# Differential attention: scaling each output tile one step later in the written order

## The chip, the cores and the metric

The kernel runs on one core of one Trainium2 chip. The metric is the device time of one execution in microseconds (us); lower is better. Every engine (TensorE, VectorE, ScalarE, GpSimd, and SyncE, which issues transfers) works through its own queue in order; semaphores tie them together.

## The reference

A two-layer decoder trunk for 512 tokens of width 1024, in float32. Layer 0 runs latent attention and differential attention side by side, then a gated feed-forward network with a short convolution; layer 1 runs two other kinds of attention and such a network again. What matters here is differential attention in layer 0: 4 heads, queries in 4 blocks of 128, value width 128.

```python
def probs(qb, kf):
    s = jnp.einsum('bhqd,bhkd->bhqk', qb, kf).astype(jnp.float32) * scale + bias
    return jax.nn.softmax(jnp.where(causal, s, -jnp.inf), axis=-1)

p = probs(a1, k1) - lam * probs(a2, k2)
return jnp.einsum('bhqk,bhkd->bhqd', p.astype(v.dtype), v)
...
o_diff = diff_attention(dq[:, :, 0], dq[:, :, 1], dk[:, :, 0], dk[:, :, 1], dv, lam,
                        alibi_slopes(DIFF_HEADS))
o_diff = rms_norm(o_diff, subln_g) * (1.0 - lam_init)
return jnp.concatenate([heads_last(o_mla), heads_last(o_diff)], axis=-1) @ w_out
```

Each row of 128 outputs of a head is divided by its root mean square and multiplied by a gain before the output projection.

## The kernel before

Nearly all the work is matrix products in three parts: each float32 matrix is split into a rounded high part (ScalarE's cast, L83) and the rest (VectorE's subtraction, L84), and `mm3` (L316) multiplies high by high, high by low and low by high. TensorE is kept supplied with such products while the attention runs.

Differential attention is written as a pipeline over 16 units, one for each head and query block, in the order of L1355: head by head, blocks 3, 2, 0, 1. The loop at L1361 has 20 steps, numbered n from 0. Within it, the order of the text is the order of the instructions on TensorE, VectorE, ScalarE and GpSimd (`manual_schedule`, L1360); nothing reorders them. In a step n:

- `score` (L1227): TensorE makes the two score blocks of unit n; VectorE adds the position bias and takes the minimum (L1246).
- a weight tile is loaded and split (`W.ahead` or `W2.next`, L1367 to L1372: L83 and L84).
- `exps` (L1250): ScalarE takes the exponentials and their sums.
- `fill` (L1344): TensorE works through ready-made products, `plan[n][0]` of them here and `plan[n][1]` further down.
- `turn` (L1263): TensorE transposes the combined probabilities of unit n - 1 (L883), ScalarE copies them out (L886).
- `value` (L1266): for unit n - 2, TensorE multiplies by the values (L1271), ScalarE scales the result into the head's tile `otok` (L1272) and sums its squares (L1275), and GpSimd makes the inverse root r: an addition (L1277) and a power (L1278). The constant it adds, `epsp`, is set once by GpSimd (L1209).
- a move: GpSimd issues one transfer of a chain that adds up feed-forward weights in DRAM (`sum_steps`, L147; the issue is L163). An earlier part of that chain, without steps of the loop in between, stands ahead of the loop in GpSimd's queue (`make_sums`, L1058 and L1059).
- `norm` (L1282): VectorE scales an earlier unit's output tile by its r and the gain, in place (L1285).
- `combine` (L1256): VectorE forms the difference of the two probability blocks of unit n (L1258 to L1260).
- in steps 7, 11, 15 and 19, `finish` (L1288): TensorE transposes the four scaled tiles of a head (L1292), ScalarE and VectorE split the result (L226, L227) for the output projection.

The steps in which an operation of a unit stands are set only by the offsets in the loop's text. `r` lies in one of four buffers of the tag `rr` (L1276), `otok` in one of two (L1229).

Of the kernel before, what the change touches and what calls it, by code (L numbers as in the profile page):

```python
# [97 lines left out]
def trunk(tc, A, out):  # L98
# [3 lines left out]
    with ExitStack() as top:  # L102
# [98 lines left out]
        units = []  # L201
# [18 lines left out]
        def gain(name, row):  # L220
            g = glob.tile([P, D], F32, tag="gain", name="gain", bufs=2)
            nc.sync.dma_start(g[:], A[name][row:row + 1, :].partition_broadcast(P))
            return g
# [628 lines left out]
        def even():  # L852
            with ExitStack() as es:
# [38 lines left out]
                with ExitStack() as e1:  # L892
# [197 lines left out]
                    def score(p2, i):  # L1090
                        w = (i + 1) * P
                        ps = [bank("s", "sps")[:, :w] for _ in range(2)]
                        for z in range(2):
                            h = 2 * p2 + z
                            PE.matmul(ps[z], mq[h][:, i * P:(i + 1) * P], mk[h][:, :w], start=True, stop=True)
                        st = sc.tile([P, 8], F32, tag="st", name="st", bufs=3)
                        s = [sc.tile([P, S], F32, tag="s", name="s", bufs=4)[:, :w] for _ in range(2)]
                        for z in range(2):
                            DVE.tensor_tensor_reduce(out=s[z], in0=ps[z], in1=mmask[:, 384 - i * P:S], scale=1.0,
                                                     scalar=3e38, op0=ALU.add, op1=ALU.min, accum_out=st[:, z:z + 1])  # L1100
                        for z in range(2):
                            ACT.activation(s[z], s[z], AF.Exp, bias=st[:, z:z + 1], scale=-1.0,
                                           accum_out=st[:, 2 + z:3 + z])
                        return s, st
# [10 lines left out]
                    def turn(p2, i, s):  # L1115
                        for z in range(2):
                            if i == 0:
                                pts[p2, z] = sc.tile([P, 1280], F32, tag="pt", name="pt", bufs=3)
                            pt = pts[p2, z]
                            tp = bank("tn"[z], "tpp", 4, P)  # L1120
                            for j in range(i + 1):
                                PE.transpose(tp[:, j], s[z][:, j * P:(j + 1) * P], ident[:])
                            for j in range(0, i + 1, 2):
                                n = min(2, i + 1 - j)
                                c = off[j] + (i - j) * P
                                d = off[j + 1] - off[j] - P
                                o = pt[:, c:c + P] if n == 1 else pt[:, c:c + 2 * d].rearrange(
                                    "p (a b) -> p a b", a=2)[:, :, 0:P]
                                t = tp[:, j] if n == 1 else tp[:, j:j + 2]
                                if z:  # L1130
                                    ACT.copy(o, t)
                                else:
                                    DVE.tensor_copy(o, t)

                    def value(p2):
                        o = bank("o", "o")
                        for j in range(NT):
                            for y in range(2):
                                h = 2 * p2 + y
                                PE.matmul(o[y * 64:(y + 1) * 64, j * P:], mv[:, j, h * 64:(h + 1) * 64],  # L1140
                                          pts[p2, y][:, off[j]:off[j + 1]], start=(j == 0), stop=(j == NT - 1))
                        return lambda: split(oM[0][:, p2], oM[1][:, p2], o)
# [19 lines left out]
                    units = [(p2, i) for p2 in range(4) for i in range(NT)]  # L1162
# [3 lines left out]
                    def fill(n):  # L1166
                        for _ in range(n):
                            next(fills.pop(0))
# [81 lines left out]
                def exps(a):  # L1250
                    e, st = a
                    for z in range(2):
                        ACT.activation(e[z], e[z], AF.Exp, bias=st[:, 1 - z:2 - z], scale=-1.0,
                                       accum_out=st[:, 3 - z:4 - z])

                def combine(a):  # L1256
                    e, st = a
                    DVE.reciprocal(st[:, 4:6], st[:, 2:4])  # L1258
                    DVE.scalar_tensor_tensor(st[:, 6:7], st[:, 4:5], st[:, 3:4], neglam[:], ALU.mult, ALU.mult)
                    DVE.scalar_tensor_tensor(e[0], e[1], st[:, 6:7], e[0], ALU.mult, ALU.add)  # L1260
                    return e[0], st
# [20 lines left out]
                def norm(h, i):  # L1282
                    def f(r):
                        o = otoks[h][:, i]
                        DVE.scalar_tensor_tensor(o, o, r[:, 0:1], subg[:], ALU.mult, ALU.mult)  # L1285
                    return f

                def finish(h):  # L1288
                    def f(_):
                        tp = bank("t", "tpo", NT, P)  # L1290
                        for i in range(NT):
                            PE.transpose(tp[:, i], otoks[h][:, i], ident[:])  # L1292
                        split(oD[0][:, h], oD[1][:, h], tp.rearrange("p a b -> p (a b)"))
                    return f
# [60 lines left out]
                units = [(h, i) for h in range(4) for i in (3, 2, 0, 1)]  # L1355
                moves = sum_steps(0, range(3, 5))
                scored, turned_, valued = {}, {}, {}
                plan = ((6, 2),) + ((2, 2),) * 11 + ((2, 1),) * 4 + ((1, 0), (1, 1), (1, 2), (0, 2))
                depth, W.depth = W.depth, 0
                with tc.manual_schedule(engines={PE.engine, DVE.engine, ACT.engine, POOL.engine}):  # L1360
                    for n in range(len(units) + 4):  # L1361
                        if n < len(units):
                            a = score(*units[n])
                        if n == 8:
                            nc.sync.dma_start(g_post[:], A["ev_post_g"][0:1, :].partition_broadcast(P))
                            g_next = gain("ffn_pre_g", 0)
                        if n in (3, 6, 9):  # L1367
                            wout.append(W2.next())
                        elif len(wout) < 4:
                            W.ahead(min(len(W.made) + 1, W.pos - len(busy) + 5))  # L1370
                        elif n == 15:
                            W.ahead(W.pos + 4)  # L1372
                        if n < len(units):
                            exps(a)
                        fill(plan[n][0])
                        if n >= 1 and n - 1 < len(units):
                            turned_[n - 1] = turn(*units[n - 1])(scored.pop(n - 1))
                        if n >= 2 and n - 2 < len(units):
                            valued[n - 2] = value(*units[n - 2])(turned_.pop(n - 2))
                            if moves:  # L1380
                                moves.pop(0)()
                        fill(plan[n][1])
                        if n >= 3 and n - 3 < len(units):
                            norm(*units[n - 3])(valued.pop(n - 3))
                        if n < len(units):
                            scored[n] = combine(a)
                        if n >= 7 and n % 4 == 3:
                            finish(n // 4 - 1)(None)
                    fill(1000)
# [36 lines left out]
        def odd(xnT, pending, order):  # L1426
            xh, xl = xnT
            with ExitStack() as es:
# [411 lines left out]
                return nx, [turn_next, turns[1]]  # L1840

        xnT = even()
        xnT = ffn(0, *xnT, False)
        xnT = odd(*xnT)
# [104 lines left out]
```

## Time and profile before

| what | us |
| --- | --- |
| median of 3 runs | 1118.72 |
| lowest and highest run | 1118.53 to 1124.62 |
| the profiled execution | 1120.18 |
| its span, first to last instruction | 1118.1 |
| first and last start of the scaling L1285 | 144.3 to 201.6 |

The profile is of one execution. Its views give each instruction's start from the beginning of the span; rows of a timeline read start, duration, engine, line, operation, output<-inputs, the tile's size, a count, and in brackets the idle time of the engine ahead of it with the instruction that ended it. PE is TensorE's matrix product, PEld its weight load, DVE VectorE, ACT ScalarE, POOL GpSimd, SP SyncE. A releaser is inferred from semaphores, so a wait for several things is put down to the last of them. TensorE's granted clock was 0.999 of full speed over the span.

### The profile page before, as it was taken

The numbers are of one execution on the slowest core, as the hardware profiler recorded it, in microseconds if no ns is written. First come the engines' busy times: TensorE is split into PE (matmuls) and PEld (weight loads), VectorE is DVE, ScalarE is ACT, GpSimd is POOL, SyncE is SP. The second block draws the span as 40 slices with busy tenths as digits, with TensorE's granted clock in tenths as the row PEclk, the third lists the DMA queues.
The fourth block names the chain that finished last, engine by engine and source line by source line (L and its number), as shares of the span: only waits on it lengthen the run. The fifth ranks groups of instructions, "written<-read, shape, count | busy, mean of one in ns | idle before, by whom it ended". The sixth has DMA issues, their size and how long they took to land.

```text
span 1118.1 us, 18149 instructions
## 1 busy us (share of the span) xinstructions
PE 1105.9 (99%) x6792; PEld 961.6 (86%) x6792; DVE 898.6 (80%) x1509; ACT 641.9 (57%) x1091; POOL 126.2 (11%) x241
## 2 busy tenths in 40 slices
PE   9999999999999999999999999999999999999997
PEld 8876667898999999887888877888999999988876
DVE  6667676488899999999874566677899999999896
ACT  5555576346666665556543554565466666656562
POOL 2311143320000000000032111013200000000002
PEclk9999999999999999999999999999999999999999
DMA  8788898457556555354738999947656565535461
GB/s 289 239 227 228 224 283 219 126 181 199 170 180 196 173 187 180 123 179 150 245 95 280 289 293 289 238 115 201 201 155 199 173 187 191 173 126 164 151 207 75
DMA packets 72599, 218.02 MB, mean 195 GB/s; under 512 B 10048, under 2 KB 11200, under 8 KB 64320
## 3 DMA queue, kind: packets, MB, share of 16 engines
q1 hardware_dynamic: 61248, 147.53, 39.9%
q0 software_dynamic: 9920, 67.12, 24.0%
q10 hardware_dynamic: 1344, 2.23, 0.6%
q8 instruction: 53, 0.87, 0.3%
q14 instruction: 34, 0.28, 0.1%
HBM read 209.47 MB, written 73.43 MB: 253 GB/s over the span
## 4 chain that ended last, share of the span: by engine, by line
PE 76%; DMA 10%; DVE 8%; issue 4%; ACT 1%; POOL 1%; SPq 0%; POOLq 0%; DVEq 0%; ACTq 0%
PE u L320 12%; PE u L318 12%; PE u L319 12%; DMA ws<-in_ffn_up_q 5%; DVE wl L84 3%; DMA ws<-ws 3%; PE apt L318 3%; PE apt L319 3%; PE apt L320 3%; PE acc L318 3%; PE acc L320 2%; PE acc L319 2%; PE ao L318 2%; PE ao L320 2%; PE ao L319 2%
## 5 line engine op out<-in xcount | busy, mean ns | idle before, releaser
L84 DVE TENSOR_TENSOR wl<-wraw,wh 128x1024 fp32r<-128x1024 f32 x246 | 298.8, 1220 | 39.8 <-ACT wh L83 39.0
L83 ACT CAST wh<-wraw 128x1024 fp32r<-128x1024 f32 x246 | 254.8, 1047 | 111.8 <-PE u L319 24.4
L320 PE MATMUL u<-xh,wl 128*128 128x256 f32 (+1 forms) x640 | 195.0, 305 | 0.0
L318 PE MATMUL u<-xh,wh 128*128 128x256 f32 (+1 forms) x640 | 194.9, 305 | 0.0
L319 PE MATMUL u<-xl,wh 128*128 128x256 f32 (+1 forms) x640 | 194.8, 304 | 0.0
L320 PEld LDWEIGHTS u<-xh,wl 128*128 128x128 f32 x640 | 122.3, 191 | 5.5 <-DVE wl L84 0.7
L319 PEld LDWEIGHTS u<-xl,wh 128*128 128x128 f32 x640 | 122.3, 191 | 5.0
L318 PEld LDWEIGHTS u<-xh,wh 128*128 128x128 f32 x640 | 122.3, 191 | 4.9
L318 PE MATMUL u<-gh,wh 128*128 128x256 f32 x384 | 108.7, 283 | 0.0
L320 PE MATMUL u<-gh,wl 128*128 128x256 f32 x384 | 108.6, 283 | 0.0
L319 PE MATMUL u<-gl,wh 128*128 128x256 f32 x384 | 108.6, 283 | 0.0
L318 PE MATMUL acc<-wh,gh 128*128 128x512 f32 (+1 forms) x234 | 90.5, 389 | 0.6 <-DVE uu L689 0.6
L319 PE MATMUL acc<-wl,gh 128*128 128x512 f32 (+1 forms) x234 | 90.9, 388 | 0.0
L320 PE MATMUL acc<-wh,gl 128*128 128x512 f32 (+1 forms) x234 | 90.7, 387 | 0.0
L233 POOL TENSOR_TENSOR rv<-ms,epst 128x1 f32<-128x1 f32 x39 | 12.8, 329 | 632.2 <-ACT junk L285 287.0
L482 ACT ACTIVATE y<-u,cw 128x512 f32<-128x512 f32 x88 | 67.8, 777 | 26.8 <-PE u L320 26.8
L319 PEld LDWEIGHTS u<-gl,wh 128*128 128x128 f32 x384 | 73.7, 192 | 0.1
L318 PEld LDWEIGHTS u<-gh,wh 128*128 128x128 f32 x384 | 73.6, 192 | 0.1
L320 PEld LDWEIGHTS u<-gh,wl 128*128 128x128 f32 x384 | 73.7, 192 | 0.0
L163 POOL DMA_DIRECT2D ws<-in_ffn_up_q x72 | 51.6, 718 | 161.8 <-DMA ws<-ws 75.0
L488 DVE SCALAR_TENSOR_TENSOR y<-u,cw,y 128x510 f32<-128x510 f32 x88 | 65.6, 747 | 2.2
L486 DVE SCALAR_TENSOR_TENSOR y<-u,cw,y 128x511 f32<-128x511 f32 x88 | 65.1, 744 | 0.9 <-ACT y L482 0.9
(374 smaller groups left out, 2495.6 us busy)
## 6 DMA issues: line engine op xcount, KB each, us to landing
ws<-in_ffn_up_q POOLq DMA_DIRECT2D x48, 768.0 KB, 12.3
wraw<-ws SPq DMA_DIRECT2D x128, 256.0 KB, 3.0
wraw<-in_ffn_up_q SPq DMA_DIRECT2D x96, 256.0 KB, 2.9
wraw<-in_ffn_w_down SPq DMA_DIRECT2D x44, 512.0 KB, 3.5
ws<-ws POOLq DMA_DIRECT2D x16, 768.0 KB, 14.2
ws<-in_ffn_up_q POOLq DMA_DIRECT2D x24, 512.0 KB, 6.2
wraw<-in_ffn_w_up SPq DMA_DIRECT2D x24, 512.0 KB, 4.5
wraw<-in_od_w_dqk SPq DMA_DIRECT2D x12, 512.0 KB, 10.3
```

The source lines that it names most:

```text
L83: self.nc.scalar.copy(h[:, :w], raw[:, :w])
L84: self.nc.vector.tensor_tensor(l[:, :w], raw[:, :w], h[:, :w].bitcast(F32), ALU.subtract)
L163: nc.gpsimd.dma_start(tiles[j][c][:].rearrange(wide, q=4), src.rearrange(wide, q=4), accum_op=op, max_dma_last_dim=8192)
L233: POOL.tensor_tensor(v[:, :n], ms, epst[:, :n], ALU.add)
L318: PE.matmul(o, lh, rh, start=first, stop=False, skip_group_check=more)
L319: PE.matmul(o, lh, rl, start=False, stop=False, skip_group_check=more)
L320: PE.matmul(o, ll, rh, start=False, stop=last, skip_group_check=more)
L482: ACT.activation(y[:, z], u[z], AF.Identity, bias=c[:, 3:4], scale=c[:, 2:3])
L486: DVE.scalar_tensor_tensor(y[:, z, 1:], u[z][:, :S - 1], c[:, 1:2], y[:, z, 1:], ALU.mult, ALU.add)
L488: DVE.scalar_tensor_tensor(y[:, z, 2:], u[z][:, :S - 2], c[:, 0:1], y[:, z, 2:], ALU.mult, ALU.add)
```

## The change

The scaling `norm` of unit n - 3 stood in step n; now it is that of unit n - 4. It stands at the same place within a step, between the second `fill` and `combine`. The first scaling moves from step 3 to step 4, the last from step 18 to step 19, where it stands just ahead of the last `finish`. The condition on the upper end is dropped, since the loop has 20 steps and n - 4 is always below 16. Nothing that is computed changes.

```diff
                         fill(plan[n][1])
-                        if n >= 3 and n - 3 < len(units):
-                            norm(*units[n - 3])(valued.pop(n - 3))
+                        if n >= 4:
+                            norm(*units[n - 4])(valued.pop(n - 4))
                         if n < len(units):
                             scored[n] = combine(a)
                         if n >= 7 and n % 4 == 3:
                             finish(n // 4 - 1)(None)
```

On VectorE the scaling of step 3 disappears and one more stands at the end; ScalarE, GpSimd and SyncE issue the same instructions in the same order. On TensorE only semaphore waits move, at three of the four finishes. The head's last unit, 4h + 3, was scaled in step 4h + 6, the step before its finish; it is now scaled in step 4h + 7, the step of its finish.

## The prediction

> **What bounds the kernel now.** I read the page's busy shares and its chain first, then what the scaling line L1285 waits for, then the timelines of VectorE, GpSimd and TensorE around the longest of those waits. Steps are numbered n = 0 to 19 as in the loop at L1361; unit n is scored in step n, and r(n) is the root that GpSimd makes for its output tile in step n + 2.
>
> ```profile
> PE 1105.9 (99%) x6792; PEld 961.6 (86%) x6792; DVE 898.6 (80%) x1509; ACT 641.9 (57%) x1091; POOL 126.2 (11%) x241
> PE 76%; DMA 10%; DVE 8%; issue 4%; ACT 1%; POOL 1%; SPq 0%; POOLq 0%; DVEq 0%; ACTq 0%
> ```
>
> TensorE is busy for 1105.9 of 1118.1 us, so 12.2 us is all that any reordering could save, over the whole program. The change lies in one stage; what counts is where TensorE stands still there. The answer on line L1285 (its count, its minimum, median and maximum in ns, and what its engine waited for):
>
> ```profile
> L1285 DVE SCALAR_TENSOR_TENSOR otok<-otok,rr,subg x16: 341/348/353, 144.3 to 201.6; 128x128 f32<-128x128 f32 x16
> its engine sat idle before it (us, times) until:
>   POOL rr L1278: 8.7, 4
> ```
>
> Four of sixteen scalings hold VectorE up, 8.7 us in all. The first is the longest. VectorE's timeline there (start, duration, operation; in brackets the idle time ahead and its releaser):
>
> ```profile
> 139.68 1.22 DVE L84 TENSOR_TENSOR wl<-wraw,wh 128x1024 fp32r<-128x1024 f32 x1
> 144.27 0.35 DVE L1285 SCALAR_TENSOR_TENSOR otok<-otok,rr,subg 128x128 f32<-128x128 f32 x1 [3.36 <-POOL rr L1278]
> 144.53 0.16 DVE L1258 RECIPROCAL st<-st 128x2 f32<-128x2 f32 x1
> 144.98 0.48 DVE L1260 SCALAR_TENSOR_TENSOR s<-s,st 128x256 f32<-128x256 f32 x1
> 145.38 0.68 DVE L1246 CUSTOM_DVE_ANT_0 s<-sps,dist 128x512 f32<-128x512 f32 x1
> ```
>
> Behind the waiting scaling of unit 0 stands the combine of step 3, whose last instruction (L1260) ends at 144.98 + 0.48 = 145.46. TensorE transposes that result in step 4:
>
> ```profile
> 144.27 0.39 PE L320 MATMUL aqk<-xh,wl 128*128 128x512 f32 x1
> 145.62 0.41 PE L883 MATMUL tpp<-ident,s 128*128 128x128 f32 x2 [0.95 <-DVE s L1260]
> ```
>
> So a VectorE wait of 3.36 us becomes a TensorE wait of 0.95 us. Why r(0) is late shows on GpSimd's timeline:
>
> ```profile
> 136.12 0.53 POOL L163 DMA_DIRECT2D ws<-ws  x1 [8.78 <-DMA ws<-in_ffn_up_q]
> 142.43 0.79 POOL L163 DMA_DIRECT2D ws<-in_ffn_up_q  x1 [5.77 <-PE aqk L320]
> 142.95 0.37 POOL L1209 MEMSET epsp<- 128x1 f32 x1
> 143.41 0.18 POOL L1277 TENSOR_TENSOR st<-st,epsp 128x1 f32<-128x1 f32 x1
> 143.67 0.56 POOL L1278 TENSOR_TENSOR rr<-st,mhalf 128x1 f32<-128x1 f32 x1
> ```
>
> GpSimd issues the weight sums one behind the other, each waiting for the one before to land. The issue at 142.43 adds to the tile that the copy issued at 136.12 fills, so it waits for that landing, whatever releaser the bracket names. Only then comes the constant, the addition and the power: r(0) is there at 143.67 + 0.56 = 144.23. That time follows the transfers, not TensorE.
>
> **The change part by part.** First the wait in step 3. VectorE's order there, before against after (- is gone, + is new; L1246 are the reductions of the scores, L84 is a weight split, L1285 the scaling of head 0's tile otok_1377, L1258 and L1259 begin the combine):
>
> ```order
>  L1246 ISA st 128x1
>  L84 TENSOR_TENSOR wl<-wraw,wh 128x1024
> -L1285 SCALAR_TENSOR_TENSOR otok_1377<-otok_1377,rr,subg 128x128
>  L1258 RECIPROCAL st<-st 128x2
>  L1259 SCALAR_TENSOR_TENSOR st<-st,neglam 128x1
> ```
>
> Step 3 has no scaling any more; every later step has one at the same place as before, one unit older; the sixteenth comes in step 19. What the combine of step 3 still needs, and what step 4 holds:
>
> ```profile
> 140.37 0.19 ACT L1253 ACTIVATION_READ_ACCUMULATOR s<-s,st 128x1 f32 x1
> 141.95 1.13 PE L1236 MATMUL sps<-dqk 64*128 64x512 f32 x4
> 146.60 1.22 DVE L84 TENSOR_TENSOR wl<-wraw,wh 128x1024 fp32r<-128x1024 f32 x1
> 147.74 0.35 DVE L1285 SCALAR_TENSOR_TENSOR otok<-otok,rr,subg 128x128 f32<-128x128 f32 x1
> 148.46 0.75 DVE L1260 SCALAR_TENSOR_TENSOR s<-s,st 128x512 f32<-128x512 f32 x1
> 150.11 0.60 PE L883 MATMUL tpp<-ident,s 128*128 128x128 f32 x4
> ```
>
> The exponentials' sums are there at 140.37 + 0.19 = 140.56, the split ends at 139.68 + 1.22 = 140.90, and the combine took 145.46 - 144.53 = 0.93 us behind the scaling (which holds the queue for 0.26, from 144.27 to 144.53). It would end near 141.9. TensorE wants the result at 144.27 + 0.39 = 144.66, 2.8 us later: the 0.95 us goes entirely.
>
> What is late next? In step 4, VectorE waits for the scores, complete at 141.95 + 1.13 = 143.08. Its two reductions took 146.60 - 145.38 = 1.22, the split 147.74 - 146.60 = 1.14 until the next start: unit 0 is scaled from about 143.08 + 2.36 = 145.4. r(0) is there 1.2 us earlier, so VectorE does not wait. From the start of the scaling to the end of the combine took 148.46 + 0.75 - 147.74 = 1.47; it ends near 146.9. TensorE's transposes of step 5 move from 150.11 to 149.16 and find it done 2.3 us before. So r(0) may come 1.2 + 2.1 = 3.3 us later than traced (0.13 of the 2.3 is the gap between VectorE's end and TensorE's weight load, taken below) before TensorE loses anything.
>
> Of the other three waits, the shortest and the last:
>
> ```profile
> 188.75 0.35 DVE L1285 SCALAR_TENSOR_TENSOR otok<-otok,rr,subg 128x128 f32<-128x128 f32 x1 [0.77 <-POOL rr L1278]
> 201.61 0.35 DVE L1285 SCALAR_TENSOR_TENSOR otok<-otok,rr,subg 128x128 f32<-128x128 f32 x1 [2.27 <-POOL rr L1278]
> ```
>
> The 0.77 of step 14 goes too, since step 14 then scales unit 10, but no TensorE wait followed it. The two of the last steps (8.7 - 3.36 - 0.77 = 4.57 together) stay, one step later, where VectorE has nothing but scalings in between. I cost both at nothing.
>
> Second, the finish. The transposes of a head (L1292) used to read a tile scaled one step earlier; now the last scaling stands in the same step, ahead of the combine. TensorE's rows in step 7, with the semaphores:
>
> ```order
>  L1292 MATMUL tpo<-ident,otok_1377 128x128 [waits Activation_49]
> -L1292 MATMUL tpo<-ident,otok_1377 128x128 x3
> -L1236 MATMUL sps<-dqk_94 128x512 [waits DVE_49] x2
> +L1292 MATMUL tpo<-ident,otok_1377 128x128 [waits DVE_49]
> +L1292 MATMUL tpo<-ident,otok_1377 128x128 x2
> +L1236 MATMUL sps<-dqk_94 128x512 x2
> ```
>
> The wait moves from the scores of step 8 to the second transpose of the finish. Behind it are queued all of TensorE's next products. Whether it costs anything is the distance between the scaling at that place and the weight loads, in steps 7, 11 and 15:
>
> ```profile
> 159.99 0.35 DVE L1285 SCALAR_TENSOR_TENSOR otok<-otok,rr,subg 128x128 f32<-128x128 f32 x1
> 160.55 0.60 PEld L1292 LDWEIGHTS tpo<-ident,otok 128*128 128x128 f32 x4
> 177.09 0.35 DVE L1285 SCALAR_TENSOR_TENSOR otok<-otok,rr,subg 128x128 f32<-128x128 f32 x1
> 178.78 0.60 PEld L1292 LDWEIGHTS tpo<-ident,otok 128*128 128x128 f32 x4
> 193.43 0.35 DVE L1285 SCALAR_TENSOR_TENSOR otok<-otok,rr,subg 128x128 f32<-128x128 f32 x1
> 194.25 0.59 PEld L1292 LDWEIGHTS tpo<-ident,otok 128*128 128x128 f32 x4
> 145.59 0.20 PEld L883 LDWEIGHTS tpp<-ident,s 128*128 128x128 f32 x2 [1.35 <-issue]
> ```
>
> The last row gives the price of passing the result on: L1260 ended at 145.46, the load began at 145.59, 0.13 later. A second transpose's load starts a quarter of 0.60, so 0.15, behind the first. The margins are 160.55 + 0.15 - 160.34 - 0.13 = 0.23 us in step 7, 178.93 - 177.57 = 1.36 in step 11 and 194.40 - 193.91 = 0.49 in step 15. In both narrow places VectorE itself starts when TensorE is done, just ahead of step 7 and in step 15:
>
> ```profile
> 156.59 0.69 DVE L1333 COPY dqk<-aqk 128x512 f32<-128x512 f32 x1 [2.00 <-PE aqk L320]
> 191.60 0.42 DVE L1246 CUSTOM_DVE_ANT_0 s<-sps,dist 128x256 f32<-128x256 f32 x1 [1.78 <-PE sps L1236]
> ```
>
> Both engines shift together, so I cost the three waits at nothing. The waiting form itself is no cost: the fourth finish has it already, and its four loads, in the fence below, take 0.59.
>
> Third, that fourth finish, in step 19, with the last root held by a transfer:
>
> ```profile
> 199.84 0.87 POOL L163 DMA_DIRECT2D ws<-in_ffn_up_q  x1 [0.89 <-DMA ws<-ws]
> 200.49 0.45 POOL L1277 TENSOR_TENSOR st<-st,epsp 128x1 f32<-128x1 f32 x1
> 202.08 0.59 PEld L1292 LDWEIGHTS tpo<-ident,otok 128*128 128x128 f32 x4
> ```
>
> The scaling ends at 201.96, so this margin is 202.08 + 0.15 - 201.96 - 0.13 = 0.14 us. If TensorE comes 0.95 earlier and this r(15) does not, 0.95 - 0.14 = 0.81 is given back. Bounds: nothing, or 0.81. I take nothing, because the transfer that holds GpSimd was itself issued behind an earlier root, r(12), which follows TensorE's products.
>
> GpSimd, ScalarE and SyncE issue the same instructions in the same order, so no DMA passes another. Sum against the profiled execution: span 1118.1 - 0.95 = 1117.15, time 1120.18 - 0.95 = 1119.2. That execution is 1.46 above the median of 1118.72; against the median the forecast is 1118.72 - 0.95 = **1117.8 us**.
>
> **The rivals.**
>
> *No gain.* GpSimd's release hangs on a chain of transfers, and executions need not agree on it. The issues of this stage:
>
> ```profile
> DMA to landing us min/median/max: 4.3/7.8/9.9
> ```
>
> If r(0) usually comes 0.95 us earlier than traced, there is nothing to remove: 1118.7. The same end, 1118.72 - 0.14 = 1118.6, is reached if the last finish gives 0.81 back. For it: these margins are set by transfers. Against: the copy issued at 136.12 was waited for during 5.77 us, already less than the median landing of 7.8. Chance 0.22.
>
> *The wait only moves.* GpSimd made r(0) while VectorE idled; now VectorE works then. The addition took 0.18 at 143.41 and this much while VectorE combined (the row at 148.46):
>
> ```profile
> 148.68 0.57 POOL L1277 TENSOR_TENSOR st<-st,epsp 128x1 f32<-128x1 f32 x1 [2.23 <-ACT jk L1275]
> ```
>
> 0.39 us more for each of three instructions is 1.2, inside the 3.3 that step 4 allows: still 1117.8. Were each held for a whole split of 1.22, r(0) would be 3.66 late, 0.3 beyond that: 1118.1. Chance 0.05. [...] The trace agrees that GpSimd slows, by 0.39 here; that it waits a whole operation these rows don't show.
>
> *Slower: TensorE waits at the finish.* The point is VectorE falling more than 0.23 us behind in step 7, or 0.49 in step 15. Splits do wait for ScalarE's cast:
>
> ```profile
> 153.36 1.22 DVE L84 TENSOR_TENSOR wl<-wraw,wh 128x1024 fp32r<-128x1024 f32 x1 [0.40 <-ACT wh L83]
> ```
>
> At 0.40 late only step 7 would lose 0.17. A whole split late, 1.22, costs 0.99 and 0.73; step 11 has none. Against the 0.95 saved that is +0.77: 1119.5. Chance 0.08.
>
> **How the numbers follow.** Forecast 0.62, no gain 0.22, moved 0.05, slower 0.08; 0.03 for what I don't see. The likeliest gives 1117.8. Downwards: the transfer issued at 136.12 took at most 142.43 - 136.12 = 6.3; where it takes the median of 7.8, the wait removed is 0.95 + 1.5 = 2.45, still within 3.3: 1116.3. Upwards: 1119.5, and the profiled execution alone lies 1.46 above the median, so 1120.2. Range 1116.2 to 1120.2. About 1%, 11 us, is what a measurement of this kernel can tell from no change; no case comes near it: same 0.97, and 0.015 each for faster and slower.
>
> **What would show it.** VectorE's combine of step 3 starting near 141 with no GpSimd wait; TensorE without the 0.95 us gap ahead of L883; L1285 waiting twice instead of four times, about 4.6 us; L1292 without idle time ahead of it. Idle time there that names VectorE proves the slower case; a wait for r(0) in step 4 that reaches L883 proves the moved one. A later stall that takes the 0.95 back, where TensorE now has no wait, would be something I have missed.

## The result and the profile after

| what | us |
| --- | --- |
| the changed kernel, median of 22 runs | 1117.62 (1116.88 to 1119.08) |
| the kernel before, 22 runs beside it | 1120.74 (1118.14 to 1124.62) |
| ratio, 95% interval | 0.9977, 0.9969 to 0.9986 |
| the profiled execution of the changed kernel | 1117.45, span 1115.3 |

The change saves 2.6 us, by the interval 1.6 to 3.5 (the ratio is taken over all the runs; the two medians alone are 3.12 us apart). The sign and the place were as predicted; the saving is larger than the 0.95 us worked out. That the predicted 1117.8 lies so near to 1117.62 is partly luck: it was counted from a median of three runs, 1118.72, and the 22 runs beside the changed kernel had 1120.74. A second comparison, further down, gave 1117.59 us and a ratio of 0.9987 (0.9973 to 1.0000), so the two comparisons put the saving at 2.6 and 1.5 us, and the second one's interval reaches down to nothing.

The page of the changed kernel, busy shares and the chain of work that ended last:

```profile
PE 1105.0 (99%) x6792; PEld 961.8 (86%) x6792; DVE 898.6 (81%) x1509; ACT 641.7 (58%) x1091; POOL 128.3 (12%) x241
PE 82%; DVE 9%; DMA 4%; issue 2%; ACT 2%; POOL 0%; SPq 0%; POOLq 0%; DVEq 0%; ACTq 0%
```

The busy times are the same work to within 2.1 us. In the chain the share of transfers fell from 10% to 4% and TensorE's rose from 76% to 82%: a stretch that had followed a transfer now follows TensorE. The scaling line, with what VectorE waited for ahead of it:

```profile
L1285 DVE SCALAR_TENSOR_TENSOR otok<-otok,rr,subg x16: 340/347/353, 145.4 to 198.7; 128x128 f32<-128x128 f32 x16
its engine sat idle before it (us, times) until:
  POOL rr L1278: 4.2, 3
```

Three waits of 4.2 us together stand where four of 8.7 us stood. VectorE in steps 3 and 4 of the changed kernel:

```profile
139.91 0.16 DVE L1258 RECIPROCAL st<-st 128x2 f32<-128x2 f32 x1
140.36 0.48 DVE L1260 SCALAR_TENSOR_TENSOR s<-s,st 128x256 f32<-128x256 f32 x1
142.20 0.69 DVE L1246 CUSTOM_DVE_ANT_0 s<-sps,dist 128x512 f32<-128x512 f32 x1 [1.35 <-PE sps L1236]
143.43 1.22 DVE L84 TENSOR_TENSOR wl<-wraw,wh 128x1024 fp32r<-128x1024 f32 x1
145.37 0.35 DVE L1285 SCALAR_TENSOR_TENSOR otok<-otok,rr,subg 128x128 f32<-128x128 f32 x1 [0.72 <-POOL rr L1278]
146.08 0.75 DVE L1260 SCALAR_TENSOR_TENSOR s<-s,st 128x512 f32<-128x512 f32 x1
```

The combine of step 3 starts at 139.91 with no wait for GpSimd and ends at 140.84. Unit 0 is scaled at 145.37, behind a new wait of 0.72 us, and the combine of step 4 ends at 146.83. GpSimd's rows beside it:

```profile
136.28 0.53 POOL L163 DMA_DIRECT2D ws<-ws  x1 [8.27 <-DMA ws<-in_ffn_up_q]
142.82 0.79 POOL L163 DMA_DIRECT2D ws<-in_ffn_up_q  x1 [6.01 <-DMA ws<-ws]
143.80 0.89 POOL L1277 TENSOR_TENSOR st<-st,epsp 128x1 f32<-128x1 f32 x1
144.77 0.56 POOL L1278 TENSOR_TENSOR rr<-st,mhalf 128x1 f32<-128x1 f32 x1
```

Here the bracket at the second issue names the landing of the copy, as the prediction had it against the bracket of before. And TensorE:

```profile
143.36 0.39 PE L320 MATMUL aqk<-xh,wl 128*128 128x512 f32 x1
143.59 0.38 PE L883 MATMUL tpp<-ident,s 128*128 128x128 f32 x2
...
148.07 0.60 PE L883 MATMUL tpp<-ident,s 128*128 128x128 f32 x4
```

The transposes of step 4 start 0.23 us behind the product ahead of them, the usual distance, and those of step 5 find a result that has been ready for 148.07 - 146.83 = 1.24 us. The gap is gone and did not reappear one step on.

What did it cost before? Start to start, 145.62 - 144.27 = 1.35 us against 0.23 now, so 1.12; the profile's 0.95 leaves out 0.17, since the end of the product ahead is modelled. The changed execution is 1120.18 - 1117.45 = 2.73 us shorter: 144.27 - 143.36 = 0.91 had already come together ahead of step 4, 1.12 is the gap, and 0.7 comes later. Of this last part the largest piece that a view names is a wait in layer 1 (total, times, longest, of before and then of the changed kernel):

```profile
PE run L1561 <- DVE z L1569: 1.1, 2, 0.9
```

```profile
PE run L1561 <- DVE z L1569: 0.4, 2, 0.2
```

In a second profile of the unedited kernel before it is 0.5, so it differs from one execution to the next without the change. The 0.91 and this 0.7 are put down to the two executions, not to the change. That leaves 1.12 us in this pair of profiles, less than the 2.6 that the runs show; the experiments are about the difference.

### The profile page after: what moved, and what is told of

It is laid out like the page before. It is cut to its first block, busy times and chain, and to the rows that moved or that the text cites. A ratio compares the mean times of both kernels' runs of the same rounds, so it can differ in the third digit from the quotient of the medians.

```text
span 1115.3 us, 18146 instructions
## 1 busy us (share of the span) xinstructions
PE 1105.0 (99%) x6792; PEld 961.8 (86%) x6792; DVE 898.6 (81%) x1509; ACT 641.7 (58%) x1091; POOL 128.3 (12%) x241
## 4 chain that ended last, share of the span: by engine, by line
PE 82%; DVE 9%; DMA 4%; issue 2%; ACT 2%; POOL 0%; SPq 0%; POOLq 0%; DVEq 0%; ACTq 0%
PE u L320 12%; PE u L319 12%; PE u L318 12%; DVE wl L84 3%; PE acc L318 3%; PE acc L319 2%; PE acc L320 2%; DMA wraw<-in_ffn_w_down 2%; PE apt L318 2%; PE ao L318 2%; PE apt L319 2%; PE apt L320 2%; PE ao L320 2%; PE ao L319 2%; DMA wraw<-in_od_w_dqk 1%
```

## The experiments

The theory at this point: r(0) is released by the landing of a transfer, and that time differs from one execution to the next, so one profile's gap is one sample; later releases make larger gaps, and perhaps something more behind them. Rivals: the later scalings or the moved end give a gain of their own, or the 22 runs beside the changed kernel happened to be long. In kernels with added lines the line numbers of the profile are shifted by a few.

**The kernel before once more, unedited.**

> The kernel before, unedited, for a second profile. Chain theory (GpSimd's transfer chain sets when r(0) is there, and the scaling of step 3 hands that on to TensorE): ratio 1.000 to itself; its TensorE gap ahead of L883 in step 4 is another one than 0.95 us, anywhere from 0 to 4 us, and its time lies above the changed kernel's by about that gap. Rival (the gain lies elsewhere, at the finishes, in step 14 or behind the stage): the gap is again near 1 us and explains less than half of the 2.6 us.

Measured: 1118.95 us, ratio 0.9991 (0.9975 to 1.0007), no difference from itself. Its profiled execution took 1122.01 us, the longest of its runs, and shows why. TensorE and GpSimd (the issue that releases r(0)):

```profile
142.75 0.79 POOL L163 DMA_DIRECT2D ws<-in_ffn_up_q  x1 [6.26 <-DMA ws<-ws]
...
143.22 0.39 PE L320 MATMUL aqk<-xh,wl 128*128 128x512 f32 x1
145.94 0.66 PE L883 MATMUL tpp<-ident,s 128*128 128x128 f32 x2 [2.33 <-DVE s L1260]
147.25 0.63 PE L319 MATMUL aqk<-xl,wh 128*128 128x512 f32 x1
147.68 0.63 PE L320 MATMUL aqk<-xh,wl 128*128 128x512 f32 x1
...
151.90 0.60 PE L883 MATMUL tpp<-ident,s 128*128 128x128 f32 x4
```

The gap is 2.33 us, start to start 2.72 - 0.23 = 2.49. Then the products come 0.43 us apart (147.68 - 147.25) where they come 0.23 apart elsewhere. The windows of the same execution (stretch and length; busy time and count of PE, PEld, DVE, ACT and POOL; granted clock; transfers' share and GB/s):

```profile
146.00:148.00 2.00, 2.00 (x7) 1.81 (x8) 2.00 (x5) 1.56 (x5) 0.77 (x2) 0.50 1.01 209
148.00:150.00 2.00, 2.00 (x8) 1.16 (x9) 1.46 (x5) 1.45 (x6) 0.91 (x2) 0.73 0.92 352
150.00:152.00 2.00, 2.00 (x13) 1.48 (x10) 1.50 (x5) 1.87 (x5) 0.76 (x2) 1.00 0.97 377
```

Around the end of the gap the granted clock fell to half (0.50 from 146 to 148), for some 3.4 us. From the transposes of step 4 to those of step 5 it took 151.90 - 145.94 = 5.96 us, against 148.07 - 143.59 = 4.48 in the changed kernel: 1.48 lost to the clock. Together 3.97 us, of the 4.56 by which this execution is longer than the changed kernel's. In the first profile of before the same distance is 150.11 - 145.62 = 4.49, with a granted clock of 1.00 from 144 to 150: there a gap of 0.95 cost no clock.

**Only the first scaling moved.** Unit 0 is scaled in step 4, together with unit 1; all others stay as before.

```diff
-                        if n >= 3 and n - 3 < len(units):
-                            norm(*units[n - 3])(valued.pop(n - 3))
+                        for u in {3: (), 4: (0, 1)}.get(n, (n - 3,)):
+                            if 0 <= u < len(units):
+                                norm(*units[u])(valued.pop(u))
```

> Only unit 0's scaling is moved from step 3 to step 4; all others and the finishes stay as before. Chain theory: all of the gain, ratio 0.9977, about 1117.6 us, no TensorE gap in step 4. Rival (gain at the finishes, in step 14 or from later semaphores): ratio 1.000, about 1120.7 us.

**All but the first moved.** Unit 0 is scaled in step 3 as before, every other one step later.

```diff
-                        if n >= 3 and n - 3 < len(units):
-                            norm(*units[n - 3])(valued.pop(n - 3))
+                        for u in {3: (0,), 4: ()}.get(n, (n - 4,)):
+                            if 0 <= u < len(units):
+                                norm(*units[u])(valued.pop(u))
```

> All scalings one step later except unit 0's, which stays in step 3. Chain theory: no gain, ratio 1.000, about 1120.7 us, the TensorE gap in step 4 as before. Rival (the gain comes from the other fifteen scalings): ratio 0.9977, about 1117.6 us.

Measured, both beside the same runs of before: the first alone 1118.21 us, ratio 0.9983 (0.9969 to 0.9998); all but the first 1118.97, ratio 0.9994 (0.9978 to 1.0009). The part of the change that counts is the first scaling, though the two intervals overlap. The profiles are plainer. With the first kept (the profiled execution, 1122.56 us, is the longest of its twelve):

```profile
143.16 0.79 POOL L163 DMA_DIRECT2D ws<-in_ffn_up_q  x1 [7.51 <-PE sps L1236]
...
143.97 0.39 PE L320 MATMUL aqk<-xh,wl 128*128 128x512 f32 x1
146.35 0.41 PE L883 MATMUL tpp<-ident,s 128*128 128x128 f32 x2 [1.99 <-DVE s L1260]
...
152.41 0.60 PE L883 MATMUL tpp<-ident,s 128*128 128x128 f32 x4
```

The gap stands, 2.15 us start to start above the usual 0.23, and 152.41 - 146.35 = 6.06 shows 1.58 of half clock behind it (the granted clock was 0.50 from 148 to 150). With only the first moved:

```profile
136.49 0.79 POOL L163 DMA_DIRECT2D ws<-in_ffn_up_q  x1 [5.67 <-DMA ws<-ws]
...
143.48 0.39 PE L320 MATMUL aqk<-xh,wl 128*128 128x512 f32 x1
143.71 0.38 PE L883 MATMUL tpp<-ident,s 128*128 128x128 f32 x2
```

No gap; but here the release came at 136.49, so early that, by the fixed distance below, the order of before would have had none either. This profile alone does not prove the cure. What it adds is the spread of the release: the same issue, on the same queue, came at 142.43, 142.75, 143.16 and 136.49. Wherever the scaling in step 3 waited for it, TensorE's transposes start a fixed time behind it: 145.62 - 142.43, 145.94 - 142.75 and 146.35 - 143.16 are each 3.19 us.

**The root taken from behind the transfer.** The scalings stay as in the kernel before; the last issue of the sum that stands ahead of the loop goes behind r(0) in GpSimd's queue.

```diff
-                        make_sums(0, range(2, 3), sums_of[0][3][1][0:1, 0:1])
+                        held = sum_steps(0, range(2, 3), sums_of[0][3][1][0:1, 0:1])
+                        with tc.manual_schedule(engines={POOL.engine}):
+                            for move in held[:-1]:
+                                move()
...
-                moves = sum_steps(0, range(3, 5))
+                moves = held[-1:] + sum_steps(0, range(3, 5))
...
-                            if moves:
+                            for _ in range(2 if n == 2 else 1):
                                 moves.pop(0)()
```

> Every scaling stays where it was before; GpSimd's last transfer issue of the part ahead of the loop (the one at 142.43) is issued behind r(0) instead of ahead of it, so r(0) no longer waits for the landing of the copy issued at 136.12. Chain theory: r(0) ready near 138 us, no VectorE wait in step 3, ratio about 0.998, 1117.6 to 1118.2 us. Rival (the place of the scaling itself matters, not the transfer): ratio 1.000.

Measured: 1117.51 us, ratio 0.9976 (0.9962 to 0.9991). GpSimd in that kernel:

```profile
136.45 0.56 POOL L1281 TENSOR_TENSOR rr<-st,mhalf 128x1 f32<-128x1 f32 x1
141.67 1.37 POOL L163 DMA_DIRECT2D ws<-in_ffn_up_q  x2 [4.66 <-DMA ws<-ws]
```

```profile
143.24 0.39 PE L320 MATMUL aqk<-xh,wl 128*128 128x512 f32 x1
143.47 0.38 PE L883 MATMUL tpp<-ident,s 128*128 128x128 f32 x2
...
144.98 0.35 DVE L1288 SCALAR_TENSOR_TENSOR otok<-otok,rr,subg 128x128 f32<-128x128 f32 x1 [0.46 <-POOL rr L1281]
```

r(0) is there at 137.01, and the transposes of step 4 follow their product at 0.23 us. The held issue waits until 141.67 with r(1) behind it; the scaling of step 4 waits 0.46 us for that root, and no TensorE gap follows in step 5. With no scaling moved, this gives what the change gives: it is the transfer ahead of r(0) that cost the time.

**The root made later on purpose, before and after.** GpSimd does some extra powers on a column that nothing else reads, just ahead of r(0); the next three runs share their runs of before with the one behind them.

```diff
+                pad = sc.tile([P, 1], F32, tag="pad", name="pad")
...
+                        if (h, i) == units[0]:
+                            for _ in range(4):
+                                POOL.tensor_tensor(pad[:], epsp[:], mhalf[:, 0:1], ALU.pow)
```

The kernel before with four powers:

> The kernel before, with four extra powers on GpSimd (4 x 0.56 = 2.2 us) directly ahead of r(0), written to a column that nothing reads. Chain theory: r(0) comes 2.2 us later and TensorE stands still 2.2 us longer in step 4; where the gap then is 2.3 us or more, its products run at half pace for some 3 us behind it, 1.3 us more: ratio 1.002 to 1.004, 2 to 4 us slower. Rival (TensorE doesn't depend on r(0) there): 1.000.

The changed kernel with four:

> The changed kernel with the same four extra powers ahead of r(0). Chain theory: VectorE's wait in step 4 grows by about 2.2 us from 0.7, but TensorE has slack there (3.3 us by the prediction, of which 0.7 + some 0.4 is used up): no TensorE gap, time as the changed kernel's, ratio 0.997 to 0.998. Rival (the wait has only moved to step 4 and reaches TensorE): about 2 us slower than the changed kernel, ratio 1.000.

The changed kernel with twelve:

> The changed kernel with twelve extra powers (12 x 0.56 = 6.7 us) ahead of r(0). Chain theory with a slack of 3.3 us: TensorE stands still in step 5 for 6.7 less some 2.2 to 3.3, so 3.4 to 4.5 us, and its clock drops behind it for 1.3 us: ratio 1.001 to 1.003, a gap ahead of L883 in step 5. Rival (slack much larger than worked out): ratio 0.998.

Measured: before with four 1123.37 us, ratio 1.0032 (1.0014 to 1.0050); changed with four 1118.46, ratio 0.9984 (0.9970 to 0.9998); changed with twelve 1124.38, ratio 1.0041 (1.0022 to 1.0060). The same delay costs the old order 3.6 us and leaves the new one faster than the undelayed kernel before. In the first of the three the profiled execution, 1118.88 us, is one of the short ones, with an early release; no profile shows one of the longer ones:

```profile
138.91 0.79 POOL L163 DMA_DIRECT2D ws<-in_ffn_up_q  x1 [5.10 <-PE tpp L883]
139.90 2.44 POOL L1280 TENSOR_TENSOR pad<-epsp,mhalf 128x1 f32<-128x1 f32 x4
...
144.51 0.41 PE L883 MATMUL tpp<-ident,s 128*128 128x128 f32 x2 [1.24 <-DVE s L1261]
```

138.91 + 3.19 + 2.44 = 144.54 against 144.51: the fixed distance holds, lengthened by the delay. In the second, the profile shows its longest execution, 1120.55 us, with the release at 144.27:

```profile
148.51 0.35 DVE L1289 SCALAR_TENSOR_TENSOR otok<-otok,rr,subg 128x128 f32<-128x128 f32 x1 [3.51 <-POOL rr L1282]
...
150.12 0.63 PE L883 MATMUL tpp<-ident,s 128*128 128x128 f32 x4 [1.54 <-DVE s L1261]
```

So the new order has an end to its slack as well, and there the wait moves to step 5, 1.54 us of it. I had expected four powers to stay inside the slack; with a release as late as this they don't. With twelve (7.95 us) it is passed by far:

```profile
151.01 0.35 DVE L1289 SCALAR_TENSOR_TENSOR otok<-otok,rr,subg 128x128 f32<-128x128 f32 x1 [6.24 <-POOL rr L1282]
...
152.63 1.09 PE L883 MATMUL tpp<-ident,s 128*128 128x128 f32 x4 [4.28 <-DVE s L1261]
```

The window in which that gap ends, in the columns of the windows above:

```profile
152.00:156.00 4.00, 3.37 (x12) 3.09 (x13) 3.93 (x13) 2.98 (x9) 3.89 (x6) 0.50 0.95 262
```

The gap is back in step 5, with the half clock behind it: from the transposes of step 5 to those of step 6 it took 6.41 us, against 3.64 in the changed kernel, 2.77 more. The ratio is a little above the one expected.

**The scaling behind the combine.** In the changed kernel `norm` stands behind `combine`, next to the finish, to see the third rival's wait at work.

```diff
-                        if n >= 4:
-                            norm(*units[n - 4])(valued.pop(n - 4))
                         if n < len(units):
                             scored[n] = combine(a)
+                        if n >= 4:
+                            norm(*units[n - 4])(valued.pop(n - 4))
                         if n >= 7 and n % 4 == 3:
```

> The changed kernel with the scaling behind the combine instead of ahead of it, so that at a finish it comes later by the combine (0.85 to 1.2 us, in step 11 some 1.6). Margins of the prediction (0.23, 1.36 and 0.49 us in steps 7, 11 and 15): TensorE waits at L1292 some 0.6, 0.2 and 0.4 us, 1.2 us in all: ratio 0.998 to 0.999, with idle time ahead of L1292 that names VectorE. Rival (the finishes have no part in the time): no idle time at L1292, ratio 0.9975.

Measured: 1118.80 us, ratio 0.9997 (0.9987 to 1.0006). TensorE's weight loads of the finishes waited for the scaling (total, times, longest):

```profile
PEld tpo L1292 <- DVE otok L1285: 1.2, 3, 0.6
```

The 1.2 us is met; singly the waits are 0.57, 0.39 and 0.29 us in steps 7, 11 and 15, where 0.6, 0.2 and 0.4 were expected. The ratio lost about 0.0010 (1.1 us) against the second comparison of the changed kernel and 0.0020 against the first, so the interval does not size it more closely than the profile.

**Both cures, and the changed kernel again.** The first of these has the edit of the root taken from behind the transfer on top of the change; the second is the changed kernel unedited.

> The changed kernel, with the last issue of chunk 2's weight sum placed behind the first root, as in the run that moved that issue alone. Theory (the gain comes only from the gap that a late r(0) made in step 4): the two cures do not add up. Ratio against before 0.997 to 0.998, the changed kernel's ratio within 0.001; r(0) ready near 137 us, VectorE's waits for rr two times instead of three (the 0.72 us of step 4 gone, about 3.5 us left), no TensorE gap above 0.5 us ahead of L883 in step 4 or 5. Rival (the order at the tail or the older scalings give a gain of their own): the two add, ratio 0.995 to 0.996.

> The changed kernel unedited, for a second profile and the same runs of before as the kernel beside it. Theory: ratio 0.997 to 0.998 again; whatever the time of GpSimd's release in its profile (136 to 145 us), no TensorE gap above 0.5 us ahead of L883 in step 4 or 5 and the granted clock 1.00 from 142 to 154 us. Rival (the first comparison caught slow runs of before): ratio 0.999 to 1.000.

Measured: both cures 1117.76 us, ratio 0.9987 (0.9973 to 1.0001); the changed kernel 1117.59, ratio 0.9987 (0.9973 to 1.0000). They do not add up: the 0.995 to 0.996 of a second gain lies outside the interval, and the kernel with both cures does not beat the changed kernel. Both ratios lie above the 0.997 to 0.998 expected, with intervals that reach into it; by this comparison alone the saving could be nothing. In the profile with both cures VectorE's wait of step 4 is gone and those of the last two steps remain:

```profile
DVE otok L1288 <- POOL rr L1281: 4.0, 2, 2.0
```

The second profile of the changed kernel has an early release, and TensorE is on time:

```profile
137.16 0.79 POOL L163 DMA_DIRECT2D ws<-in_ffn_up_q  x1 [6.20 <-PE sps L1236]
...
143.25 0.38 PE L883 MATMUL tpp<-ident,s 128*128 128x128 f32 x2
```

The runs themselves show the same from outside. Over all comparisons, on several chips:

| us | lowest | a quarter below | median | a quarter above | highest |
| --- | --- | --- | --- | --- | --- |
| before, 111 runs | 1116.33 | 1118.27 | 1119.44 | 1120.92 | 1126.32 |
| changed, 34 runs | 1116.88 | 1117.21 | 1117.62 | 1118.23 | 1121.42 |

The two medians are 1.82 us apart. The best executions of before are as short as those of the changed kernel. The change does not lower the floor; it takes away the long executions. The latest release, 144.27, would by the fixed distance have made a gap of 144.27 + 3.19 - 143.95 = 3.51 us in the old order (143.95 is when TensorE began the transposes there). With gaps of 0 to 3.5 us and a further 1.5 behind the larger ones, a spread of about 5 us is what the release explains; the tenth of its runs above 1122.6 is not explained by anything profiled here.

## Why the prediction was right, and what it mis-sized

*What bounds, and where.* Right. The wait of VectorE for r(0) in step 3 became TensorE's gap, and the transfer ahead of r(0) made it late: taking the root from behind that transfer gives the same time without moving a scaling.

*The gap goes entirely.* Right in place, mis-sized as a term. The sum took off 0.95 us, the idle time of one execution. Two things were missing. The lost time is counted from start to start: 1.12 there. And the gap is a sample: 2.49 and 2.15 in the other two profiles with the first scaling in step 3 and a late release, each with about 1.5 us of half clock behind it, so 3.97 and 3.73 in all, and nothing where the release is early. The downward case of the prediction allowed for a later landing, 1.5 us more, but its price had no clock in it; and it was held to be an end of the range where it is common. The changed kernel's own first profile has such a release: 142.82 + 3.19 = 146.01 in the old order, which would have held TensorE 146.01 - 143.59 = 2.42 us. Worked out so for all ten profiles whose queue ahead of that point is unedited, the old order's gap is nothing in three, 0.74 and 1.12 us in two and 2.15 to 3.51 in five, 1.47 on average; with 1.5 of half clock behind each of the five that makes 2.2 us. This is an estimate, since only three of the ten had the first scaling in step 3 without a delay; it lies between the 1.5 and 2.6 that the two comparisons gave. The downward case also looked for the spread in the wrong place: it let the last copy take longer to land, 7.8 us for 6.3. From that copy's issue to the release it took 5.63 to 8.04 us in the ten profiles, but its issue itself came between 130.28 and 137.70, so most of the spread lies ahead of it in the chain.

*The combine near 141, from 140.56.* It ran from 139.91, earlier, because this execution was 0.9 us ahead there; no GpSimd wait, as said.

*The rival "no gain".* It is right for single executions: with an early release the old order has no gap, by the fixed distance, and 1116.33 is the lowest time of before. It does not hold for the median.

*The rival "the wait only moves".* It happened, harmlessly. The addition took 0.89 us where it took 0.18 before, and ended at 144.69, 0.04 us behind the split that ended at 143.43 + 1.22 = 144.65: it lasted until that VectorE operation was done. The prediction's own row shows the same, though it was read as 0.39 of slowing: that addition ended at 148.68 + 0.57 = 149.25, 0.04 behind L1260, which ended at 148.46 + 0.75 = 149.21. The term of 3.66 us, a whole split of 1.22 for each of the three instructions, no run shows: here the addition alone took longer, by 0.71, and the constant and the power took 0.37 and 0.56 us, as before. With the later release this cost a VectorE wait of 0.72 us in step 4. Of the 3.3 us of slack that the prediction gave step 4, about 1.1 was left (1.24, less 0.13 to pass the result on): r(0) came 1.10 later than traced, 145.33 against 144.23, and TensorE's transposes of step 5 came 1.09 earlier than the 149.16 worked out. The delayed kernels show the slack's end: beyond it the gap opens in step 5.

*The finish.* Right: in steps 7, 11 and 15 the margins were 0.22, 1.35 and 0.49 us, against 0.23, 1.36 and 0.49. The changed kernel's rows in steps 7 and 19:

```profile
157.93 0.35 DVE L1285 SCALAR_TENSOR_TENSOR otok<-otok,rr,subg 128x128 f32<-128x128 f32 x1
158.48 0.59 PEld L1292 LDWEIGHTS tpo<-ident,otok 128*128 128x128 f32 x4
...
198.71 0.35 DVE L1285 SCALAR_TENSOR_TENSOR otok<-otok,rr,subg 128x128 f32<-128x128 f32 x1 [1.44 <-POOL rr L1278]
200.04 0.59 PEld L1292 LDWEIGHTS tpo<-ident,otok 128*128 128x128 f32 x4
```

In numbers, the margin in step 7 is 158.48 + 0.15 - 158.28 - 0.13 = 0.22 us, and no idle time stands ahead of L1292. In step 19 it is 200.19 - 199.06 - 0.13 = 1.00, not 0.14, and 0.42 in the second profile of the changed kernel: the scaling came 2.90 us earlier than before and TensorE 2.04, so the 0.81 was not given back, as taken. Whether r(15) came early for the reason that the prediction gave, r(12) ahead of its transfer, was not tried. Where the margin is used up, as with the scaling behind the combine, TensorE does wait, 1.2 us in all there.

*L1285's waits.* Two of 4.6 us were predicted, and none in step 4; three of 4.2 came, the third being the 0.72 of step 4.

## What to carry to other kernels

A wait that a transfer ends is one sample in each profile; here the same release spread over 7.8 us. Look at the spread of the runs and at a second profile before pricing it by one. Count a gap of the bounding engine from start to start and look at the granted clock in the windows behind it. An in-place step that waits for a slow neighbour is best put where something else is already late; moving it cost nothing here because its last reader, the finish, kept its margin (0.22 us at the narrowest), and that margin can be read off the trace.

## What was unexpected of the hardware

TensorE's granted clock fell to half at gaps as short as 1.99 us. In six profiles with a gap ahead of L883, it stayed at 1.00 for idle times of 0.95, 1.24 and 1.54 us and fell to 0.50 for 1.99, 2.33 and 4.28. Worked out from the mean clocks of the windows around it (0.94, 0.92 and 0.96 where it begins, 0.71, 0.73 and 0.69 where it ends, each taken as one step between 1.00 and 0.50), the fall came 3.4, 2.1 and 3.3 us behind the start of these three idle times, in the first of them when TensorE had been at work again for 1.4 us; and the half clock lasted 3.4, 3.4 and 6.8 us, the last twice the others. It cost 1.58, 1.48 and 2.77 us on top of the gap. One more idle time, 1.68 us near the start of the kernel with the root taken from behind the transfer, left TensorE's pace as it was: behind it the products of L938 follow each other at 10.82, 11.20 and 11.58, 0.38 us apart, as in the changed kernel (10.99, 11.37 and 11.74), which idled 0.33 there. Where between 1.68 and 1.99 it starts, or whether it depends on more than the length, these profiles don't settle.

The other is the spread of a chained transfer: in the ten profiles whose queue ahead of that point is unedited, the same issue of GpSimd was released between 136.49 and 144.27 us. What sets the landings along the chain was not tried.
